# A decoder trunk whose TensorE warm-up gains 95 products of zeros, read in nineteen patterns

## The chip, the cores and the metric

The kernel runs on one core of a Trainium2 chip. The metric is the device time of one execution in microseconds (us), on the slowest core, which here is the only one. Times of the kernel before: median 978.93 us of 2 runs (978.71 to 979.16).

## The reference

Two layers of a decoder trunk act on a sequence of 256 tokens, 1024 wide, all in float32. Each layer is a SwiGLU feed-forward half step, a token mixer beside a 4-head cross-attention into 256 memory tokens, and a second SwiGLU half step; each is added to the scaled input and normalised.

```
for l in range(2):
    x = LN(alpha*x + 0.5*swiglu(x, gate[l,0], up[l,0], down[l,0]))      # 1024 -> 2816 -> 1024
    u = x @ (w_in_conv if l == 0 else w_in_mlstm)
    tok = short_conv_mixer(u) if l == 0 else mlstm_mixer(u)
    xa = memory_cross_attention(u[..., -256:], mem @ w_kv_mem[l])
    x = LN(alpha*x + concat(tok, xa) @ w_out[l])
    x = LN(alpha*x + 0.5*swiglu(x, gate[l,1], up[l,1], down[l,1]))
```

`swiglu(x, g, u, d)` is `(silu(x @ g) * (x @ u)) @ d`. The products of zeros that this study is about are no part of it: nothing reads their result.

## The kernel before

All weights stream once from the chip's memory, in pieces of 128x2048 float32 (1 MB), in the order in which they are used (`pieces`). One engine each does one thing. SyncE issues the transfers (L131, L135, L163). ScalarE (ACT) rounds a landed piece to float32r, the form that TensorE takes in one pass, and writes it to a tile `wh`; VectorE (DVE) subtracts, and writes the rest to `wl` (`split`, L101 and L102). Activations are split in the same way into two halves. TensorE (PE) then makes three products for each pair of blocks, high by high, high by low and low by high (`mm3`, L182 to L184), or two with the high and low activations side by side as 512 moving columns (`mmw`, L190). Each product loads its 128x128 block (the held operand) and streams 256 to 512 columns past it (the moving operand).

Three landing buffers (`rawp`) and five pairs of split buffers (`wp`) limit how far transfers and splits run ahead of PE. A scheduler sets the order of instructions on each engine from the order of the code and its own estimates; engines meet only through semaphores.

The start is the place of the change. While the first transfers are under way, DVE writes zeros into a tile `warm` (L148), and PE makes 18 products of it (L150, L151), 128x128 held against 256 moving columns, into a PSUM bank that nobody reads. GpSimd (POOL) meanwhile writes `mhalf` and the identity; ACT loads a table for Silu and applies it once to a column of `mhalf` (L160), so that the table is there later. Then come eight transfers `xw` of the input with the first weight pieces (L163), each split by ACT and DVE as it lands, and the first feed-forward group `gu` on PE (L190), whose products for each of the 8 blocks of the input wait for that block's split. The first group makes 64 products of this kind, and so does the next.

## Time and profile before

| | |
|---|---|
| median of 2 runs | 978.93 us |
| the profiled execution | 979.45 us |
| its span, first to last instruction | 977.0 us |
| PE busy | 967.6 us, 5266 products |
| PE weight loads busy | 831.0 us |
| DVE busy | 663.3 us |
| ACT busy | 527.0 us |
| POOL busy | 20.5 us |
| mean granted TensorE clock | 0.999 |
| memory read | 185.01 MB, 190 GB/s over the span |

The profiled execution took 2.45 us more than its span, which lies before the first and after the last recorded instruction. "PE" rows are products, "PEld" rows the loads of held operands, which run beside the products before them. Products overlap in a pipeline: the duration of one is longer than the step from its start to the next one's start, so a price per product is read from the steps between starts, and not from the durations.

### The profile page before, as it was taken

The page shows a single profiled execution, that of the slowest core. Times are in us where ns is not written, and L with a number is a line of the kernel's source. Part 1 is how long each engine was busy: PE and PEld are TensorE (multiplying, and loading weights), DVE is VectorE, ACT ScalarE, POOL GpSimd, SP SyncE. Part 2 cuts the span into 40 slices and gives each one's busy share as a digit, 9 for nine tenths or more (in the row PEclk, how much of TensorE's full clock was granted, in tenths as well). Part 3 has the DMA queues.
Part 4 walks back from the last instruction along what each step waited for, and adds up shares of the span by engine and source line. Part 5 has one row for each costly group of instructions (what it writes and reads, how often), then busy time and mean ns, then how long its engine had stood idle before and what let it go on. Part 6 is the DMA issues. An engine that isn't in the chain of part 4 may idle for free.

```text
span 977.0 us, 13255 instructions
## 1 busy us (share of the span) xinstructions
PE 967.6 (99%) x5266; PEld 831.0 (85%) x5266; DVE 663.3 (68%) x1016; ACT 527.0 (54%) x847; POOL 20.5 (2%) x32
## 2 busy tenths in 40 slices
PE   9999999999999999999999999999999999999997
PEld 8888888888888888888888888889998788888885
DVE  7675657869677755656875656568697786565565
ACT  7665555457535555555444555545875345555540
POOL 0000000000000000000000000001000000000000
PEclk9999999999999999999999999999999999999999
DMA  8784646466445654646375464633646446546421
GB/s 314 295 311 159 218 170 215 173 226 214 167 169 178 247 201 150 222 166 215 133 286 184 164 224 149 229 114 111 234 162 215 158 167 248 203 146 221 164 87 43
DMA packets 28141, 186.91 MB, mean 191 GB/s; under 512 B 3504, under 2 KB 3504, under 8 KB 7216
## 3 DMA queue, kind: packets, MB, share of 16 engines
q1 hardware_dynamic: 27792, 185.55, 53.3%
q8 instruction: 41, 0.67, 0.3%
q10 hardware_dynamic: 288, 0.52, 0.1%
q14 instruction: 20, 0.16, 0.1%
HBM read 185.01 MB, written 1.05 MB: 190 GB/s over the span
## 4 chain that ended last, share of the span: by engine, by line
PE 95%; DVE 2%; ACT 1%; DMA 1%; issue 0%; SPq 0%; DVEq 0%
PE gu L190 43%; PE y L182 8%; PE y L184 8%; PE y L183 8%; PE gx L182 2%; PE gx L184 2%; PE gx L183 2%; PE cx L190 2%; PE cb L190 2%; PE cg L190 2%; PE yo L182 1%; PE yo L184 1%; PE yo L183 1%; PE kb L190 1%; PE xq L190 1%; PE xt L255 1%
## 5 line engine op out<-in xcount | busy, mean ns | idle before, releaser
L102 DVE TENSOR_TENSOR wl<-raw,wh 128x1024 fp32r<-128x1024 f32 x334 | 394.7, 1207 | 143.6 <-ACT wh L101 142.9
L101 ACT ACTIVATE wh<-raw 128x1024 fp32r<-128x1024 f32 x334 | 333.2, 1043 | 139.3 <-PE y L184 63.4
L190 PE MATMUL gu<-x,wh 128*128 128x512 f32 x1216 | 388.6, 395 | 0.0
L190 PEld LDWEIGHTS gu<-x,wl 128*128 128x128 f32 x1216 | 228.3, 188 | 52.1 <-DVE wl L102 0.8
L190 PE MATMUL gu<-x,wl 128*128 128x256 f32 x1216 | 242.8, 278 | 0.3 <-DVE wl L102 0.2
L190 PEld LDWEIGHTS gu<-x,wh 128*128 128x128 f32 x1216 | 189.5, 189 | 3.7 <-ACT wh L101 0.2
L182 PE MATMUL y<-wh,h 128*128 128x512 f32 (+1 forms) x352 | 137.4, 390 | 0.0
L183 PE MATMUL y<-wl,h 128*128 128x512 f32 (+1 forms) x352 | 136.6, 388 | 0.0
L184 PE MATMUL y<-wh,h 128*128 128x512 f32 (+1 forms) x352 | 136.5, 389 | 0.0
L195 DVE TENSOR_TENSOR s<-s,gu 128x256 f32<-128x256 f32 x152 | 63.1, 418 | 101.9 <-ACT s L194 101.7
L194 ACT ACTIVATE s<-gu 128x256 f32<-128x256 f32 x152 | 57.6, 382 | 102.9 <-PE gu L190 102.9
L184 PEld LDWEIGHTS y<-wh,h 128*128 128x128 f32 x352 | 66.1, 188 | 14.2 <-DVE h L326 0.4
L183 PEld LDWEIGHTS y<-wl,h 128*128 128x128 f32 x352 | 66.1, 188 | 13.6
L182 PEld LDWEIGHTS y<-wh,h 128*128 128x128 f32 x352 | 66.1, 188 | 12.9 <-ACT h L325 0.7
L325 ACT ACTIVATE h<-s 128x256 fp32r<-128x256 f32 x76 | 31.8, 419 | 65.9 <-DVE s L322 65.9
L321 ACT ACTIVATE s<-s 128x256 f32<-128x256 f32 x76 | 31.7, 417 | 38.0 <-DVE s L195 38.0
L326 DVE TENSOR_TENSOR h<-s,h 128x256 fp32r<-128x256 f32 x76 | 32.1, 422 | 17.3 <-ACT h L325 17.1
L182 PE MATMUL gx<-wh,x 128*128 128x512 f32 x96 | 38.1, 396 | 0.3 <-ACT x L284 0.3
L184 PE MATMUL gx<-wh,x 128*128 128x512 f32 x96 | 37.4, 391 | 0.0
L183 PE MATMUL gx<-wl,x 128*128 128x512 f32 x96 | 37.4, 390 | 0.0
L322 DVE SCALAR_TENSOR_TENSOR s<-s 128x256 f32<-128x256 f32 x76 | 32.0, 421 | 1.4
L449 PE MATMUL qkp<-x,wh 128*128 128x256 f32 x96 | 27.4, 286 | 0.0
(223 smaller groups left out, 967.9 us busy)
## 6 DMA issues: line engine op xcount, KB each, us to landing
raw<-in_wgu SPq DMA_DIRECT2D x83, 1024.0 KB, 4.8
raw<-in_wd SPq DMA_DIRECT2D x43, 1024.0 KB, 4.8
raw<-in_wconv SPq DMA_DIRECT2D x10, 1024.0 KB, 4.8
raw<-in_wout SPq DMA_DIRECT2D x8, 1024.0 KB, 4.8
raw<-in_wm SPq DMA_DIRECT2D x7, 1024.0 KB, 4.9
gb<-in_lngb SPq DMA_DIRECT2D x6, 1024.0 KB, 4.8
raw<-in_wkv SPq DMA_DIRECT2D x4, 1024.0 KB, 4.7
raw<-in_wop SPq DMA_DIRECT2D x4, 776.0 KB, 4.5
```

The costliest lines, as they stand in the source:

```text
L101: act.activation(h, raw, AF.Copy)
L102: dve.tensor_sub(l, raw, h.bitcast(F32))
L182: pe.matmul(o, ah, bh, start=start, stop=False)
L183: pe.matmul(o, ah, bl, start=False, stop=False)
L184: pe.matmul(o, al, bh, start=False, stop=stop)
L190: pe.matmul(o, w[part], b, start=(k, part) == (0, 0), stop=(k, part) == (KC - 1, 0))
L194: act.activation(o, bank[:, T:], AF.Copy)
L195: dve.tensor_add(o, o, bank[:, :T])
L321: act.activation(t_[:, :256], t_[:, :256], AF.Silu)
L322: dve.scalar_tensor_tensor(t_[:, 256:], t_[:, :256], 0.5, t_[:, 256:], op0=ALU.mult, op1=ALU.mult)
L325: act.activation(hh, t_[:, 256:], AF.Copy)
L326: dve.tensor_sub(hT[g][:, 1, fc, :], t_[:, 256:], hh.bitcast(F32))
```

## The change

The tile `warm` was a 128x256 corner of an activation buffer; now the whole buffer of 4096 columns is filled with zeros, the first 256 columns by DVE as before, the other 3840 by POOL. After the 18 products of before, PE makes 95 more into the same PSUM bank, in nineteen forms of five products each. Fifteen forms have 256 moving columns: the held operand is plain (128 columns side by side), broadcast (one column read 128 times, step 0), shifted by 4, 8, 16 or 128 columns, or read with a step of 2, 4, 8, 16 or 31 columns; the moving one lies at the start of the buffer or at column 2048, plain or with a step of 2 or 4. Four forms have 512 moving columns, with the held operand plain, broadcast, and with steps 2 and 16.

```
-    warm = new_act("warm")[:, 0, 0]
+    wt = new_act("warm").rearrange("p k c t -> p (k c t)")
+    warm = wt[:, :T]
     dve.memset(warm.bitcast(F32), 0.0)
+    pool.memset(wt[:, T:].bitcast(F32), 0.0)
     wb = mbank("warm")
     for _ in range(WARM):
         pe.matmul(wb[:, :256], warm[:, :P], warm, start=True, stop=True)
+    mv = wt[:, 2048:2048 + T]
+    plain = wt[:, :P]
+    forms = [(plain, warm), (wt[:, :1].to_broadcast([P, P]), warm),
+             (wt[:, :1].to_broadcast([P, P]), mv), (plain, mv)]
+    forms += [(wt[:, n:n + P], mv) for n in (4, 8, 16, 128)]
+    forms += [(wt[:, :P * n:n], mv) for n in (2, 4, 8, 16, 31)]
+    forms += [(plain, wt[:, 2048:2048 + 2 * T:2]),
+              (plain, wt[:, 2048:2048 + 4 * T:4])]
+    for w_, m_ in forms:
+        for _ in range(5):
+            pe.matmul(wb[:, :256], w_, m_, start=True, stop=True)
+    for w_ in (plain, wt[:, :1].to_broadcast([P, P]), wt[:, :P * 2:2], wt[:, :P * 16:16]):
+        for _ in range(5):
+            pe.matmul(wb, w_, wt[:, 2048:2560], start=True, stop=True)
```

PE's rows at the start of the program, with their waits. Before: the 18 products of `warm`, then the first group `gu`, of input `x` and the first weight piece `wh`, `wl`.

```order
L151 MATMUL warm<-warm 128x256 [waits DVE_49]
L151 MATMUL warm<-warm 128x256 x17
L190 MATMUL gu_0_00_182<-x_109,wh_110 128x512 [waits DVE_49,Activation_49]
L190 MATMUL gu_0_01_185<-x_109,wh_110 128x512
L190 MATMUL gu_0_10_188<-x_109,wh_110 128x512
L190 MATMUL gu_0_11_191<-x_109,wh_110 128x512
L190 MATMUL gu_0_00_182<-x_109,wl_111 128x256 [waits DVE_49]
```

The same place of the changed program:

```order
L153 MATMUL warm<-warm 128x256 [waits DVE_49]
L153 MATMUL warm<-warm 128x256 x17
L164 MATMUL warm<-warm 128x256 x10
L164 MATMUL warm<-warm 128x256 [waits Pool_49]
L164 MATMUL warm<-warm 128x256 x64
L167 MATMUL warm<-warm 128x512 x20
L206 MATMUL gu_0_00_278<-x_205,wh_206 128x512 [waits DVE_49,Activation_49]
L206 MATMUL gu_0_00_278<-x_205,wl_207 128x256 [waits DVE_49]
L206 MATMUL gu_0_01_281<-x_205,wh_206 128x512
```

The 95 products stand between the old warm-up and the first product of the model, and the eleventh of them waits for POOL's zeros. Within the first groups the same products come in another order; from the third group of the first feed-forward on, PE's order is that of before.

ACT's first rows before: the table, `mhalf`, then the splits of the landed blocks `xw`.

```order
L160 ACT_TABLE_LOAD
L160 ACTIVATE mhalf<-mhalf 128x1 [waits Pool_49]
L101 ACTIVATE x_109<-xw_114 128x256 [waits DMAHW0_49]
L101 ACTIVATE wh_110<-xw_114 128x512
L101 ACTIVATE x_109<-xw_115 128x256 [waits DMAHW1_49]
```

And in the changed program:

```order
L101 ACT_TABLE_LOAD
L101 ACTIVATE x_205<-xw_210 128x256 [waits DMAHW0_49]
L176 ACT_TABLE_LOAD
L176 ACTIVATE mhalf<-mhalf 128x1 [waits Pool_49]
L101 ACTIVATE wh_206<-xw_210 128x512
```

The first split now stands ahead of `mhalf`, and a second table load stands between them. Later ACT and DVE also make the splits of the next three weight pieces ahead of the first group's gate work; the orders of the two programs join again some 70 rows on. POOL's row of 3840 zeros stands ahead of its `mhalf` and identity. SyncE's order is unchanged.

## The prediction

> **What bounds the kernel now.** I read the page's busy times first, then the chain that ended last, then the groups with the idle time before them.

> ```profile
> span 977.0 us, 13255 instructions
> PE 967.6 (99%) x5266; PEld 831.0 (85%) x5266; DVE 663.3 (68%) x1016; ACT 527.0 (54%) x847; POOL 20.5 (2%) x32
> ...
> PE 95%; DVE 2%; ACT 1%; DMA 1%; issue 0%; SPq 0%; DVEq 0%
> ...
> L190 PE MATMUL gu<-x,wh 128*128 128x512 f32 x1216 | 388.6, 395 | 0.0
> ```

> PE is busy for 967.6 of 977.0 us, the chain is PE for 95% of the span, and the largest group has no idle time before it. So what is put on PE's queue ahead of the model's first product moves the end by its whole length, except for idle time that PE has behind it now and that the later start would fill. Where that idle time is, the stretches show (us, then PE busy with its count, PEld, DVE, ACT, POOL, granted clock, DMA share, GB/s):

> ```profile
> 5.20:14.00 8.80, 8.55 (x46) 7.08 (x47) 7.61 (x15) 6.55 (x15) 0.00 (x0) 1.00 0.96 325
> 14.00:30.00 16.00, 16.00 (x91) 13.86 (x90) 13.84 (x22) 12.76 (x23) 0.00 (x0) 1.00 0.97 365
> 30.00:100.00 70.00, 70.00 (x370) 59.95 (x369) 47.75 (x65) 41.93 (x64) 0.00 (x0) 1.00 0.67 244
> ```

> Transfers are busy for 0.96 to 0.97 of the first 30 us, yet from 14 us on PE is busy all the time: what it needs has always landed. Only between 5.2 and 14 us does it idle. The order of time for PE's products and for its loads, which carry the waits, says for what:

> ```profile
> 1.18 4.00 PE L151 MATMUL warm<-warm 128*128 128x256 f32 x18 [1.18 <-DVE warm L148]
> 5.20 1.16 PE L190 MATMUL gu<-x,wh 128*128 128x512 f32 x4
> ...
> 5.17 0.76 PEld L190 LDWEIGHTS gu<-x,wh 128*128 128x128 f32 x4 [0.19 <-ACT wh L101]
> ...
> 6.84 0.19 PEld L190 LDWEIGHTS gu<-x,wl 128*128 128x128 f32 x1 [0.22 <-DVE wl L102]
> ...
> 8.99 0.19 PEld L190 LDWEIGHTS gu<-x,wl 128*128 128x128 f32 x1 [0.54 <-DVE wl L102]
> ```

> The old warm-up ends almost as the first split piece is ready, at 5.17 us. Up to 9 us PE then waits three times for a split, 0.19 + 0.22 + 0.54 = 0.95 us in all. This is everything that a later start can win back: all later waits come after PE's own work of the same stage, and move with it.

> **The change, part by part.** The first term is 75 products of 256 columns, each with its own load. The nearest rows are the projection `qkp`, a stream of just this kind, and `negm`, whose held operand is a broadcast column, as in two of the forms at 256 and one at 512:

> ```profile
> 700.02 0.28 PE L449 MATMUL qkp<-x,wh 128*128 128x256 f32 x1
> 700.14 0.28 PE L450 MATMUL qkp<-x,wh 128*128 128x256 f32 x1
> ...
> 701.09 0.28 PE L449 MATMUL qkp<-x,wh 128*128 128x256 f32 x1
> ...
> 711.09 1.07 PE L688 MATMUL negm<-eh,pick 128*128 128x256 f32 x8
> ```

> From 700.02 to 701.09 us lie nine steps, 1.07 / 9 = 0.119 us each. The eight of `negm` take 1.07 us, of which the last is 0.28: (1.07 - 0.28) / 7 = 0.113 us. I take 0.119 for all 75, since most forms have plain or stepped loads: 75 x 0.119 = 8.93 us.

> The second term is 20 products of 512 columns. The last down-projection shows such a stream:

> ```profile
> 965.17 0.39 PE L184 MATMUL y<-wh,h 128*128 128x512 f32 x1
> ...
> 966.53 0.39 PE L184 MATMUL y<-wh,h 128*128 128x512 f32 x1
> ```

> Six steps in 1.36 us are 0.227 us each: 20 x 0.227 = 4.54 us. [...]

> No row shows an operand read with a step of 2 to 31 columns. At the lower end such a read costs what a plain one does, or the broadcast's 0.113 us. For the upper end I take a read at half the rate, which the trace shows in another way: the first warm-up products, while the array still ran slowly, in the window from 2 to 4 us.

> ```profile
> 1.77 2.55 PE L151 MATMUL warm<-warm 128*128 128x256 f32 x11
> ...
> L151 PE MATMUL warm<-warm 128*128 128x256 f32 x18 | 4.0, 410 | 1.2 <-DVE warm L148 1.2
> ```

> Eleven products take 2.55 us, the last about 0.41: (2.55 - 0.41) / 10 = 0.214 us. At that price the 35 products with a step (25 in the held operand, 10 in the moving one) cost 35 x 0.095 = 3.3 us more. I take the plain price, the row they are nearest to: a load runs beside the product ahead of it, and shows only when it lasts longer than that product's step. For the same reason stepped loads beside 512 columns stay hidden even at twice their time, as 0.214 is under 0.227.

> The zeros on POOL come next, since PE's eleventh new product waits for them. POOL wrote `ident` at the start and `eh` later:

> ```profile
> 0.75 0.21 POOL masks.py:197 MEMSET ident<- 128x128 f32 x1
> ...
> L630 POOL MEMSET eh<- x1: 527/527/527, 627.9 to 627.9; 128x512 f32 x1
> ```

> That is (0.527 - 0.21) / 384 = 0.83 ns a column; 3840 columns take an estimated 0.21 + 3712 x 0.00083 = 3.3 us, from 0.72 us, when POOL's first row of the body starts, to about 4.0 us. Without its wait PE would have been through with the old warm-up at 5.17 - 0.19 = 5.0 us, so it comes to the eleventh new product at about 5.0 + 10 x 0.119 = 6.2 us. The wait is over 2 us earlier, and costs nothing; were POOL slower than that, each us beyond 6.2 would count in full.

> POOL's `mhalf` now comes after the zeros, and ACT applies Silu to it behind its first split, with a second table load:

> ```profile
> 0.72 1.28 ACT L160 ACT_TABLE_LOAD   x1 [0.72 <-PEq L913]
> 2.02 0.20 ACT L160 ACTIVATE mhalf<-mhalf 128x1 f32<-128x1 f32 x1
> 4.17 0.42 ACT L101 ACTIVATE x<-xw 128x256 fp32r<-128x256 f32 x1 [1.96 <-DMA xw<-in_xw]
> ...
> 15.71 1.06 ACT L101 ACTIVATE wh<-raw 128x1024 fp32r<-128x1024 f32 x1 [0.20 <-DMA raw<-in_wgu]
> ```

> So every split behind the first comes about 1.28 + 0.20 = 1.5 us later, and with it DVE's rests and the transfers into the buffers that they free. The cover is the new warm-up itself: the model's first product now starts at about 5.0 + 8.93 + 4.54 = 18.5 us. By then even the second group's first piece, last split on ACT at 15.71 us before, is ready, and it is needed only after the first group's eleven us of products. Without the new products the 1.5 us would count almost in full. The three pieces that ACT and DVE now split ahead of the first group's gate work stand in front of it in a queue that has nothing else to do; the fourth needs a buffer which PE frees halfway through the first group, well before the gate work is due. None of it reaches PE.

> **The sum:** 8.93 + 4.54 - 0.95 = 12.5 us. On the profiled execution's 979.45 us that is 992.0. It ran 0.5 us above the median of the runs shown, 978.93, on which the sum gives 991.4; I put 991.5. With 0.113 us for every 256 columns, and the same saving for 512 (0.216), it is 8.48 + 4.32 - 0.95 = 11.9 us, 990.8; with the 3.3 us for steps it is 994.7. About 2%, or 19.6 us, is what a measurement of this kernel can tell from no change, so the forecast is slower by 1.3%, inside that bound.

> **The rivals.** *Far steps are read at half the rate.* [...] This would apply to 20 products with held steps of 4, 8, 16 and 31, and to 5 with moving step 4: 25 x 0.095 = 2.4 us more, 993.9. For it speaks that every product of the kernel reads its columns side by side, or one column over and over, so that no row excludes it; against it that loads have some slack beside the stream. [...] If step 2 pays as well, it is the 994.7 above. Chance of these together 0.14.

> *Steps collapse the rate.* If each stepped element costs several reads, say four times the 0.119 us, the 35 products cost 35 x 0.36 = 12.6 us more and the 10 with stepped loads before 512 columns 10 x 0.25 = 2.5: 1006.5, slower by over 2%. It decides from 7.1 us over the sum, a mean of 0.28 us a stepped product. Against it stands the broadcast, the one unusual pattern in the trace, which costs less than a plain one. Chance 0.06.

> *POOL is late.* If 3840 columns go at the rate of its product `og` rather than of its short fills, PE waits.

> ```profile
> L622 POOL TENSOR_TENSOR og<-og,hnb 128x768 f32<-128x768 f32 x2 | 3.7, 1847 | 12.2 <-ACT og L621 12.2
> ```

> At 1.847 us for 768 columns the zeros end at about 0.72 + 9.2 = 9.9 us, 3.7 us after PE wants them: 995.2. That row reads two operands, a fill reads none. Chance 0.04.

> *The start is fed by transfers, and the new products are hidden.* The transfers' 0.97 up to 30 us would suit this: if PE caught up with them later, the 12.5 us would be filled from waits that go, and the time would be 979, not slower. It needs PE waits of 12.5 us behind the start; the stretches from 14 to 100 us show none. Chance 0.03.

> *The change does not do what it says:* repeated loads of the same block, five times each, might be dropped. The rows of before show 18 loads for 18 equal products, and without loads the stream would still last about its columns: 990.8, inside the range. Chance 0.03.

> **How the numbers follow.** The forecast has 0.70. The range from 990.3 to 995.5 takes in both ends of the price, the half-rate steps and POOL's wait, with 0.3 us for the spread of the runs; about 0.2 of the chance lies outside it: the collapse, the hidden start, and odds and ends of the rest. Faster by over 2% has 0.01 (nothing in the change takes work away), slower by over 2% 0.07 (the collapse and a little), within 2% the other 0.92.

> **What would show it.** In the changed profile the 75 products should step at 0.113 to 0.12 us and the 20 at about 0.227, the first `gu` product should start near 18.5 us, and the three waits for splits before 9 us should be gone. POOL's fill should take about 3.3 us, with no PE wait behind it. ACT should have two table loads. From the first group on, PE should run as before, 12.5 us later. The prediction is wrong if the forms differ by more than the bounds allow, or if PE idles after its later start.

## The result: 994.69 us, 1.6% slower

The changed kernel takes 994.69 us (median of 2 runs, 994.29 to 995.09) against 978.93: a ratio of 1.0161, 95% interval 1.0144 to 1.0178, or 15.8 us more. One execution of the all-plain kernel below took 5601 us and is left out of its numbers. The time is inside the stated range and 3.2 us over the stated 991.5. The profile's execution ran 995.09 us, with a span of 993.3, 16.3 more than before; 1.8 us of its time lie outside the span, where before 2.45 did. First the page: busy times and the chain that ended last.

```profile
span 993.3 us, 13448 instructions
PE 984.5 (99%) x5361; PEld 848.2 (85%) x5361; DVE 662.9 (67%) x1016; ACT 528.4 (53%) x848; POOL 23.7 (2%) x33
...
PE 99%; DVE 0%; ACT 0%; issue 0%; DVEq 0%
```

PE's busy time grew by 16.9 us, ACT's by 1.4 (a second table load of 1.28), and DVE's stayed. PE's start in order of time:

```profile
1.18 4.21 PE L153 MATMUL warm<-warm 128*128 128x256 f32 x18 [1.18 <-DVE warm L149]
5.18 13.36 PE L164 MATMUL warm<-warm 128*128 128x256 f32 x75
18.36 4.82 PE L167 MATMUL warm<-warm 128*128 128x512 f32 x20
23.02 0.39 PE L206 MATMUL gu<-x,wh 128*128 128x512 f32 x1
```

From start to start the 75 products take 18.36 - 5.18 = 13.18 us and the 20 take 23.02 - 18.36 = 4.66. The model begins at 23.0 us, not at 18.5. The stretch of each form shows why; each row is four products of one form (the fifth shares its window with the form before):

```profile
5.39 1.05 PE L164 MATMUL warm<-warm 128*128 128x256 f32 x4
...
7.97 0.64 PE L164 MATMUL warm<-warm 128*128 128x256 f32 x4
...
10.93 0.64 PE L164 MATMUL warm<-warm 128*128 128x256 f32 x4
...
11.64 1.11 PE L164 MATMUL warm<-warm 128*128 128x256 f32 x4
...
12.82 1.13 PE L164 MATMUL warm<-warm 128*128 128x256 f32 x4
...
16.28 1.10 PE L164 MATMUL warm<-warm 128*128 128x256 f32 x4
...
17.43 1.11 PE L164 MATMUL warm<-warm 128*128 128x256 f32 x4
...
22.09 1.10 PE L167 MATMUL warm<-warm 128*128 128x512 f32 x4
```

A row's time less its last product's own time (0.28 us where the step is short, about 0.40 where it is long), over the products but one, is the step (elsewhere below the last product's own time is 0.34 us at steps of 0.174, 0.63 at 0.45, and 0.23 for bfloat16 at 128 columns). In order: plain, 0.21 us; plain, 0.120; held step 2, 0.120; held step 4, 0.236; held step 8, 0.243; moving step 2, 0.23; moving step 4, 0.23; 512 columns with held step 16, 0.235, as plain ones. So two things were dearer than in the sum. Ten of the 75 ran before 7.2 us, where the steps shorten from 0.213 to 0.120 us (2.09 us for 10 x 0.119, 0.9 more). And 30 stepped products took double: from start to start the 20 with held steps of 4 and up took 4.66 us for 2.38, the 10 with moving steps 2.29 for 1.19, 3.4 us more together.

The point where the steps shorten is called the rise of the clock in the expectations, and "the rise" below. That is my reading: the granted clock of this profile is 1.00 in every stretch of its first 9 us. For it speaks one stretch of the run on what a read fetches, where the granted clock is 0.50 and 256-column products step at 0.213 us as well (last section).

POOL's fill was done when the estimate had it, and ACT's second table load fell beside the warm-up:

```profile
0.72 3.30 POOL L150 MEMSET warm<- 128x3840 f32 x1 [0.29 <-POOLq L929]
...
4.77 1.28 ACT L176 ACT_TABLE_LOAD   x1
6.07 0.20 ACT L176 ACTIVATE mhalf<-mhalf 128x1 f32<-128x1 f32 x1
```

What is won back shows in the starts, before and after, of the nineteenth product of the model in PE's order and of the last. In both kernels nine of the eighteen products ahead of the nineteenth are 512 columns wide. Before, with two waits of ACT that the next paragraph needs:

```profile
7.27 0.42 ACT L101 ACTIVATE x<-xw 128x256 fp32r<-128x256 f32 x1 [1.21 <-DMA xw<-in_xw]
...
9.22 0.39 PE L190 MATMUL gu<-x,wh 128*128 128x512 f32 x1
...
732.27 2.02 ACT L101 ACTIVATE wh<-raw 128x1024 fp32r<-128x1024 f32 x2 [1.48 <-DMA raw<-in_wout]
...
969.51 0.28 PE L184 MATMUL ylast<-wh,h 128*128 128x256 f32 x1
```

After:

```profile
26.19 0.39 PE L206 MATMUL gu<-x,wh 128*128 128x512 f32 x1
...
746.03 3.19 ACT L101 ACTIVATE wh<-raw 128x1024 fp32r<-128x1024 f32 x3
...
985.74 0.28 PE L200 MATMUL ylast<-wh,h 128*128 128x256 f32 x1
```

The first product came 17.8 us later (23.02 for 5.20), the nineteenth 17.0, the last 16.2. The first 0.9 us are the waits for splits, which are gone. The other 0.7 came back in the middle of the second layer, at its scores, where ACT in the profile of before had waited 1.48 us for a piece of `w_out`; that wait is there in some of the executions below (1.27 us in the changed kernel once more, 1.35 in the fill without the products) and not in others (all plain, eight more). The waits at the start differ between executions too: in the profile of before ACT waited 1.21 us for the third block of the input, until 7.27 us, and the first split of the changed kernel began at 4.34 us in this profile and at 4.04 in its next one.

### The profile page after: what moved, and what is told of

Same layout as the page of the kernel before. It is cut to its first block, busy times and chain, and to the rows that moved or that the text cites. A ratio compares the mean times of both kernels' runs of the same rounds, so it can differ in the third digit from the quotient of the medians.

```text
span 993.3 us, 13448 instructions
## 1 busy us (share of the span) xinstructions
PE 984.5 (99%) x5361; PEld 848.2 (85%) x5361; DVE 662.9 (67%) x1016; ACT 528.4 (53%) x848; POOL 23.7 (2%) x33
## 4 chain that ended last, share of the span: by engine, by line
PE 99%; DVE 0%; ACT 0%; issue 0%; DVEq 0%
PE gu L206 43%; PE y L198 8%; PE y L200 8%; PE y L199 8%; PE gx L198 2%; PE gx L200 2%; PE gx L199 2%; PE cx L206 2%; PE cb L206 2%; PE cg L206 2%; PE yo L198 1%; PE yo L200 1%; PE yo L199 1%; PE warm L164 1%; PE qkp L465 1%; PE qkp L466 1%
## 5 line engine op out<-in xcount | busy, mean ns | idle before, releaser
L102 DVE TENSOR_TENSOR wl<-raw,wh 128x1024 fp32r<-128x1024 f32 x334 | 394.5, 1207 | 149.7 <-ACT wh L101 149.1
L101 ACT ACTIVATE wh<-raw 128x1024 fp32r<-128x1024 f32 x334 | 332.8, 1043 | 143.5 <-PE y L200 65.4
```

Source lines behind the costliest of these rows:

```text
L101: act.activation(h, raw, AF.Copy)
L102: dve.tensor_sub(l, raw, h.bitcast(F32))
```

## The experiments

My theory once the result was known, A: reads with steps take double, and the late rise does the rest. The rival, B: the patterns cost nothing, and a long warm-up is slow for other reasons.

### All 95 products plain

```
-    for w_, m_ in forms: ...            # 15 forms x 5
+    for _ in range(75):
+        pe.matmul(wb[:, :256], plain, mv, start=True, stop=True)
-    for w_ in (plain, ...): ...         # 4 forms x 5
+    for _ in range(20):
+        pe.matmul(wb, plain, wt[:, 2048:2560], start=True, stop=True)
```

> All 95 new products are plain (held side by side, moving side by side), as many and as wide as in the change. Theory A (reads with steps take double): 75 steps at about 0.118 us and 20 at 0.233 us, 13.5 us in all and 1 us more if the clock rises as late as in the changed kernel; the first gu product starts at 18.5 to 19.5 us instead of 23.0, and the time is 3.4 us under the changed kernel's, about 991. Theory B (the patterns cost nothing, and the excess is the late clock and traffic on the memory): the first gu product still starts at 22 to 23 us, time about 994.5.

Ratio to the kernel before 1.0121 (1.0104 to 1.0137), 990.4 to 992.0 us. Then once more, and its profile is the one shown:

> The 95 plain products once more, for a profile of an undisturbed execution and a second interval. Theory A: 75 steps at 0.118 to 0.120 us but for those before the clock rises (0 to 10 of them at 0.213), 20 at 0.235, first gu product between 18.5 and 19.5 us, time about 991. Theory B: first gu product at 22 to 23 us.

Ratio 1.0125 (1.0110 to 1.0141), median 991.13 us.

```profile
5.18 9.62 PE L157 MATMUL warm<-warm 128*128 128x256 f32 x75
14.64 4.72 PE L159 MATMUL warm<-warm 128*128 128x512 f32 x20
19.20 0.39 PE L198 MATMUL gu<-x,wh 128*128 128x512 f32 x1
```

The model begins at 19.2 us, 3.8 earlier than in the changed kernel, and the steps shorten 1.0 us sooner (6.2 for 7.2). The time falls by 3.6 us. A stands, B falls: plain products cost what the rows of before said, and the patterns 3.4 us; the other 0.4 of the 3.8 is the earlier rise. The prediction's own sum without patterns, 991.5, is met within 0.4 us, with the late rise and a win-back larger than its 0.95 about cancelling.

### The changed kernel once more

> The changed kernel as it is, on the same chip as the others. Time 994 to 995.5. The products that step at 0.213 us at the start are those before the clock rises: if that point lies in a window that runs free of the kernel, it differs from the 7.2 us of the first profile (anywhere between about 4.5 and 8 us), and the first gu product starts up to 1.2 us earlier than 23.0; if the fill or the longer warm-up delays the clock, it is 7.2 us again. The 0.78 us wait of PE in the mLSTM scores, which was in the profile of before and not in that of the change, is not expected.

994.83 us, ratio 1.0157 (1.0142 to 1.0172). The model begins at 22.47 us: here only about four of the new products ran at 0.213 us. Over nine profiles, those of the next section not among them, in all of which PE starts at the same 1.18 us, the steps shorten at 4.3, 4.8, 5.4, 5.7, 5.8, 6.0, 6.2, 7.0 and 7.2 us. The first two are the kernels without POOL's fill, all others have it, so that a free point and a delay by the fill were both open; the next runs tell them apart. My expectation of the scores' wait was a miss: ACT waited 1.27 us for `w_out` here too.

### Does the fill hold the clock back?

The kernel before with 27 more plain products and no fill, three times (F: the point runs free of the kernel; G: POOL's fill holds the clock back):

```
+    for _ in range(27):
+        pe.matmul(wb[:, :256], warm[:, :P], warm, start=True, stop=True)
```

> The kernel before with 27 more plain products and no fill on POOL (45 in all). So far the clock rose at 4.3 and 4.8 us in the two profiles without the fill, and at 5.4 to 7.2 us in the seven with it. Theory F (the point runs free of the kernel): each of three executions of this kernel has its own point between 4.3 and 7.6 us, and at least one lies beyond 5.2. Rival G (POOL's fill of 3.3 us holds the clock back): all three rise before 5.2 us. In either case the model's first product starts at 8.2 us, plus 0.094 us for each of the new products that runs before the rise.

> The second execution of the kernel with 45 plain products and no fill: a point of its own between 4.3 and 7.6 us by theory F, before 5.2 us by rival G.

> The third: a point of its own between 4.3 and 7.6 us by theory F, before 5.2 us by rival G.

PE's start in the first, up to 9 us, and in the second:

```profile
5.18 4.02 PE L153 MATMUL warm<-warm 128*128 128x256 f32 x25
```

```profile
4.78 3.40 PE L153 MATMUL warm<-warm 128*128 128x256 f32 x27
8.02 0.40 PE L192 MATMUL gu<-x,wh 128*128 128x512 f32 x1
```

The steps shorten at 7.1, 4.3 and 5.3 us, and the model begins at 9.28, 8.02 and 8.48. One kernel shows nearly the whole spread, without the fill: F holds, G falls. The twelve points lie between 4.3 and 7.2 us, 2.9 us apart at most; what sets them is not shown. The times, 982.4 to 983.0 us in one execution each, are over what 3.2 us of products less 0.9 of waits would give. A late rise is part of it, and a wait that was not there before, for a down-projection, 1.2, 1.2 and 0.4 us in the three profiles; the row is the second's. It goes back to a transfer: ACT waited 1.63, 1.61 and 0.90 us for the piece `memT`, for which it had not waited before. In the first profile that piece was split 6.8 us after its issue (157.08 to 163.92 us), before after 5.1 (153.85 to 158.96). Why it landed later is open; these three ran on another chip than the other experiments.

```profile
PE y L184 <- ACT h L327: 1.2, 1, 1.2
```

### The fill without the products

```
-    for w_, m_ in forms: ...
-    for w_ in (plain, ...): ...
```

> POOL's fill of 3840 columns stays, the 95 products are left out. Theory A (the products are the whole cost, the cover hides the rest): without the cover ACT's late splits (second table load 1.28 us and the Silu 0.20 us) come to light, the first gu product starts near 6.8 us instead of 5.2, and the time is 1 to 1.5 us over the kernel before, about 980. Rival: the fill and the table load delay nothing that counts: time as before, 979.

980.09 us, ratio 1.0010 (1.0000 to 1.0019).

```profile
6.60 1.19 PE L192 MATMUL gu<-x,wh 128*128 128x512 f32 x4 [1.22 <-ACT wh L101]
...
4.53 1.28 ACT L162 ACT_TABLE_LOAD   x1
```

The late split appears as it was priced: the model begins 1.4 us later, at 6.60. But 0.5 of that is won back by the nineteenth product (10.12 for 9.22), and the time rises by some 0.8 us, by the interval between 0 and 1.9. That "almost in full" was probably too much: the same waits that a late start fills were there to take part of it.

### Eight more plain products, no fill

```
+    for _ in range(8):
+        pe.matmul(wb[:, :256], warm[:, :P], warm, start=True, stop=True)
```

> The kernel before with 8 more plain products of zeros and no fill (26 instead of 18). Theory A (a delay of the first gu product counts, except for the 0.95 us of waits behind it): the first gu product starts 0.9 to 1.7 us later than 5.2, by how late the clock rises; of that 0.87 us are won back by 9.2 us, and the time is 0 to 0.8 us over the kernel before. Rival (the start is fed by transfers and hides more than its waits): the delay is gone by 20 us even where it is 1.7. Rival (a longer warm-up pays, as more of the model's products run at the full clock): the time is lower than before.

979.65 us, ratio 1.0006 (0.9997 to 1.0015): no difference that this can tell, between 0.3 us less and 1.5 us more.

```profile
4.82 1.12 PE L153 MATMUL warm<-warm 128*128 128x256 f32 x8
5.78 0.40 PE L192 MATMUL gu<-x,wh 128*128 128x512 f32 x1
...
6.01 0.42 ACT L101 ACTIVATE x<-xw 128x256 fp32r<-128x256 f32 x1
...
8.94 0.39 PE L192 MATMUL gu<-x,wh 128*128 128x512 f32 x1
```

The start is 0.6 us later, and the nineteenth product 0.3 us earlier than before (8.94): 3.2 us lie between them for 4.0. More was won than the delay, so filled waits are not all of it: here the third block had landed when ACT came to it, at 6.01 us, for which it waited until 7.27 in the profile of before. How much a delay can win back thus differs with the landing of the first transfers. That a delay of 0.6 us is free is not shown, as the interval holds both nothing and 0.6 us; no version came out that beats both kernels.

### Where the price of a step begins

This run and the next two, of one execution each, make 30 plain products and then eight of each form; they took 1002.3, 1005.0 and 1002.2 us, and only the steps between their products are read.

```
+    forms = [(wt[:, :P * n:n], mv) for n in (1, 2, 3, 4, 5, 6, 8)]
+    forms += [(plain, wt[:, :1].to_broadcast([P, T]))]
+    forms += [(plain, wt[:, 2048:2048 + T * n:n]) for n in (1, 2, 3, 4, 8)]
```

> Instead of the 95: 30 plain products, then 8 of each form with 256 moving columns: held steps 1, 2, 3, 4, 5, 6, 8 (moving plain), then moving broadcast, and moving steps 1, 2, 3, 4, 8 (held plain). Theory A1 (a held column is read once in the time in which two moving ones are; a read fetches 16 bytes, and the next read of the same 16 bytes is free): held 0.118 us at steps 1 and 2, in between at step 3 (about 0.16, as every fourth read or so falls in a line that is still there), 0.235 from step 4 on. Rival A2 (any step over 2 takes a second read): 0.235 already at step 3. Moving: broadcast 0.113 to 0.118, step 1 0.118, steps 2, 3, 4 and 8 all 0.22 to 0.235 by the first trace (a moving pair must lie within 8 bytes); rival: step 8 more than step 4.

Seven of the eight products a row: held steps 2, 3, 4 and 8, moving broadcast, moving steps 2, 3 and 8.

```profile
9.95 1.00 PE L163 MATMUL warm<-warm 128*128 128x256 f32 x7
...
10.96 1.38 PE L163 MATMUL warm<-warm 128*128 128x256 f32 x7
...
12.40 1.80 PE L163 MATMUL warm<-warm 128*128 128x256 f32 x7
...
17.95 1.85 PE L163 MATMUL warm<-warm 128*128 128x256 f32 x7
...
19.75 0.95 PE L163 MATMUL warm<-warm 128*128 128x256 f32 x7
...
21.68 1.77 PE L163 MATMUL warm<-warm 128*128 128x256 f32 x7
...
23.50 1.77 PE L163 MATMUL warm<-warm 128*128 128x256 f32 x7
...
27.17 1.70 PE L163 MATMUL warm<-warm 128*128 128x256 f32 x7
```

Held: 0.120, 0.174, 0.234, 0.241. Step 3 takes three quarters of step 4, where three of four columns lie in other 16 bytes than the column before, and at step 4 every one: A1's 0.16 is near, A2's 0.235 falls. That reads go by 16 bytes is an assumption of A1 which these steps fit and do not show. Moving: broadcast 0.113, steps 2, 3 and 8 at 0.227, 0.227 and 0.217, with no growth.

### What a read fetches

The forms here are pairs and fours of float32r, held step 8 beside 256 to 512 columns, and bfloat16 operands.

```
+    pairs = wt[:, 2048:2560].rearrange("p (n f) -> p n f", f=4)[:, :, :2]
+    quads = wt[:, 2048:2560].rearrange("p (n f) -> p n f", f=8)[:, :, :4]
+    w16 = wt.bitcast(BF16)
```

> Which rule a stepped read follows. 30 plain products, then 8 of each form. Theory A3 (the moving side fetches 8 bytes at a time, a pair of float32, at one fetch for each two columns of the plain stream; the held side takes one column at a time and pays again when it enters another 16 bytes): moving pairs (two of every four columns) 0.118 us, four of every eight 0.118, moving plain from an odd column 0.118 to 0.24 (open), held step 2 from an odd column 0.118; held step 8 against 256, 384 and 512 columns 0.24, 0.24 and 0.24, as the load sets the step; in bfloat16 moving steps 2, 4 and 8 are 0.12, 0.225, 0.225 and held steps 2, 4, 8, 16 are 0.12, 0.12, 0.235, 0.235. Rival A4 (a step in elements costs, whatever its bytes): pairs about 0.17, bfloat16 moving step 2 0.225 and held step 4 0.235. Rival A5 (the 16-byte rule alone, on both sides): pairs 0.118, bfloat16 moving steps 2 and 4 0.12, 8 0.225.

In order: moving pairs, moving fours, held step 8 with 512 columns, then bfloat16 moving steps 2, 4 and 8.

```profile
11.74 1.79 PE L175 MATMUL warm<-warm 128*128 128x256 f32 x7
...
13.49 0.99 PE L175 MATMUL warm<-warm 128*128 128x256 f32 x7
...
19.52 1.87 PE L175 MATMUL warm<-warm 128*128 128x512 f32 x7
...
22.23 0.96 PE L175 MATMUL warm<-warm 128*128 128x256 bf16 x7
...
23.23 1.76 PE L175 MATMUL warm<-warm 128*128 128x256 bf16 x7
...
25.27 3.34 PE L175 MATMUL warm<-warm 128*128 128x256 bf16 x7
```

Pairs take 0.230 and fours 0.118, so A3, with its fetch of 8 bytes, falls; a moving operand that begins at an odd column takes 0.123. In bfloat16 the steps 2, 4 and 8, with four, two and one columns in each 16 bytes, take 0.114, 0.226 and 0.45: A4 and A5 fall too. Divided by the groups of 16 bytes that the 256 columns touch, that is 1.77 ns a group at step 4 (0.226 / 128) and 1.76 at step 8 (0.45 / 256). Held bfloat16 steps 8 and 16 take 0.109, where A3 had 0.235. Held step 8 in float32r takes 0.245 beside 512 columns, a little over the plain 0.23, so a load of this kind can set the step even there; step 16 in the changed kernel did not (0.235).

### The theory of 16 bytes

```
+    split4 = wt[:, 2050:2050 + 512].rearrange("p (n f) -> p n f", f=8)[:, :, :4]
+    forms = [(plain, wt[:, 2048:2560], wb), (b16, m16, wb), (plain, split4, o4)]
```

(and moving steps 5 to 7, and held steps against only 128 columns, so that the load shows)

> A theory formed after the runs before this one: each time a read enters another 16 bytes it costs about 1.8 ns, on the moving and on the held side, and the longest of that, of the array's own step (0.43 ns a moving column) and of one load sets the step between products. 30 plain products, then 8 of each form. Expected: 512 columns in float32r 0.227 to 0.235 us (128 lines of 1.8 ns), in bfloat16 0.216 (64 lines, so the array sets it); float32r in runs of four of every eight columns that begin in the middle of 16 bytes 0.226 (two lines for each four columns), where the aligned runs took 0.121; moving steps 5, 6 and 7 in float32r 0.22 to 0.235 like steps 3, 4 and 8, which the theory does not explain (it would want 0.45). With only 128 moving columns, where the load shows: held float32r steps 1, 2, 3, 4 at 0.11, 0.118, 0.173 and 0.235; held bfloat16 at 0.055 for step 1, and if the line rule holds there too 0.06 at 2, 0.115 at 4, 0.23 at 8 and at 16. Rival: loads in bfloat16 are fetched in another way, and stay at or under 0.11 at every step. Rival for the whole: the difference between 0.113 and 0.119 is not the lines but traffic of the other engines; then bfloat16 at 512 columns takes 0.227 to 0.235 too, and the run that begins in mid-line 0.121.

In order: float32r and bfloat16 with 512 columns, fours that begin in the middle of 16 bytes, bfloat16 held step 8, float32r held step 3.

```profile
9.28 1.77 PE L170 MATMUL warm<-warm 128*128 128x512 f32 x7
11.11 1.67 PE L170 MATMUL warm<-warm 128*128 128x512 bf16 x7
12.81 1.78 PE L170 MATMUL warm<-warm 128*128 128x256 f32 x7
...
21.26 0.60 PE L170 MATMUL warm<-warm 128*128 128x128 bf16 x7
...
24.20 1.38 PE L170 MATMUL warm<-warm 128*128 128x128 f32 x7
```

0.230 for float32r and 0.215 for bfloat16 at the same 512 columns; fours from the middle of 16 bytes 0.227 where aligned ones took 0.118; held step 3 again 0.174. These numbers of the theory hold, and its rival about traffic falls. Held bfloat16 stays at 0.063 even at step 8, where 128 columns at 1.76 ns would be 0.225: the theory does not hold for held bfloat16, as the other rival had it. Nor does it hold for moving float32r from step 3 on: steps of 5, 6 and 7 took 0.23, 0.226 and 0.22 where it wants 0.45. Why these, and 3, 4 and 8, stop at double where bfloat16 goes to four times is left open.

## Why the prediction was right, and where it was off

**The bound** held: PE is the chain, and what stands ahead of its first product moves the end, less the waits behind. **The plain price** held: 0.119 us and 0.227 us forecast, 0.118 to 0.120 and 0.233 measured. **POOL's fill** (3.3 us) and the **cover** for ACT's late splits held; without the cover the 1.5 us were 1.4 at the start, and some 0.8 in the time. **The win-back** of 0.95 was 0.9 at the start. But that this was "everything that a later start can win back" did not hold: another 0.7 came from a wait that differs between executions.

**Mis-sized was the price of a step**, taken as plain because a load "shows only when it lasts longer than that product's step". That fits the runs, but the load was longer than the step: with held steps of 4 columns and more the products step at 0.22 to 0.24 us, over the 0.119, and held step 8 takes the same 0.243 to 0.245 beside 256, 384 and 512 columns. And I had put the moving side with the held one, where step 2 costs double already (0.227 for 0.118). Together 3.4 us, for nothing in the sum and 3.3 at the upper end, which priced 35 products at 0.214 where 30 took 0.23. By its own signs, too, the forecast missed here: the first product of the model began at 23.0 us and not near 18.5, and the dearest form, at 0.243 us, lies over the 0.214 of the bounds. **Not in the sum was the late rise**: ten new products at 0.213 us cost 0.9 us in the one profile of the changed kernel, four cost 0.4 in the next. By terms: 13.5 + 3.4 + 0.9 - 1.6 = 16.2, as the start of the last product says; the medians differ by 15.8.

The rival of half-rate reads, held at 0.14 with its step 2, is what came true in the main: held step 2 stayed free (0.120), and moving step 2 did not (0.227). Its half rate is the 0.214 us of the slow first products; that reads pay from step 4 on was an estimate, as no row of before has a step. The runs have 0.174 us at held step 3 and 0.234 at 4. The rival would have given 994.7 at the outer end; that 994.69 meets this so closely is luck, since the late rise's 0.9 us and the 0.7 won back later are not in it. The collapse of the rate did not come; 7.1 us over its 35 products would be 0.20 us more each, 0.32 in all, and not the 0.28 that the prediction names.

## What to carry to other kernels

Price an instruction put ahead of a saturated engine at its full step, and win back only the waits that stand behind it now: here 17.8 us at the start became 16.2 at the end. Where an operand's read has a pattern that no row shows, measure it before taking the plain price because the read runs beside something else: here held steps of 2, 3 and 4 columns took 0.120, 0.174 and 0.234 us, and moving step 2 took 0.227. And what a delay at the start wins back depends on when the first transfers land, which differs from one execution to the next (the first split of the changed kernel began at 4.34 and at 4.04 us): read it from more than one profile.

## What the runs showed of the hardware

The granted clock fell although PE was never idle. In the run on what a read fetches, bfloat16 products of 0.45 us each fill the stretch before 27.5 us; then the granted clock (the third figure from the right) is halved for 3.4 us:

```profile
24.80:27.50 2.70, 2.70 (x7) 0.70 (x6) 0.08 (x1) 0.00 (x0) 0.00 (x0) 1.00 0.73 250
27.50:30.90 3.40, 3.40 (x15) 2.05 (x14) 0.00 (x0) 0.00 (x0) 0.00 (x0) 0.50 0.97 406
```

Inside that stretch, from 28.62 to 30.32 us, eight bfloat16 products of 256 columns (held steps of 2, the last of 4) take 1.70 us, 0.213 each, where those with held steps of 8 and 16 just behind it, at a granted clock of 0.99, take 0.109:

```profile
28.62 1.70 PE L175 MATMUL warm<-warm 128*128 128x256 bf16 x7
...
30.32 1.22 PE L175 MATMUL warm<-warm 128*128 128x256 bf16 x7
```

The granted clock was 0.50 in the run on the theory of 16 bytes too, from 26.3 to 29.7 us, after 128-column products that step at 0.17 to 0.24 us. In nearly 7 us of doubled 256-column products in the changed kernel (11.4 to 18.4 us) it stayed at 1.00. What brought it down is not shown. The three differ in how much of the time columns stream: taking 0.109 us for 256 bfloat16 columns and 0.055 for 128, an estimate from their steps, that is about a quarter of the time in the first case, a quarter to a third in the second, and half in the third; no run tried the amounts between.
